# A weight-row sum for attention's values moved into the down stage of the layer before

## The chip, the cores and the metric

The kernel runs on one core of a Trainium2 chip. The metric is the device time of one execution in microseconds (us). Engines are PE (TensorE, matmuls), DVE (VectorE), ACT (ScalarE), POOL (GpSimd) and SP (SyncE, which only issues DMAs here). POOL issues DMAs as well, among them all that add to their destination (`accum_op`).

## The reference

Two layers on `x` (512 rows, width 1024): layer 0 mixes by causal pooling, layer 1 by differential attention with 8 heads, and each is followed by a SwiGLU feed-forward network (FFN) of width 2816.

```
x <- LayerNorm(ALPHA * x + mixer(x));  x <- LayerNorm(ALPHA * x + ffn(x))
attention: q, k, v = split(x @ w_qkv)
  p_c = softmax(q_c k_c^T / 8 + bias[head], causal), c = 0, 1
  o = (p_0 - lam * p_1) @ v;  o <- o * rsqrt(mean(o^2) + eps) * subln_g * (1 - lambda_init);  o @ w_o
ffn: (silu(x @ w_gate) * (x @ w_up)) @ w_down
```

All is float32. The kernel splits each float32 operand into a high and a low part and makes three matmuls for one product.

## The kernel before, in words

The order of all work is written by hand: each engine runs its instructions in program order, and waits stand where a tile isn't ready. [...]

**Weights.** All weights lie in `wall`, in rows of 128 x 1024. `fetch` (L107) loads a row into a `raw` tile on SP's queue (5 buffers). `ready(n)` (L126) splits the next rows up to number n into a pair h, l (6 buffers): ACT casts the high part, DVE subtracts for the low part. For the rows in `by_dma` (most of q's and k's) ACT writes the high part and minus the raw row, and POOL adds the row by an accumulating DMA (L135). Each split also fetches the row five further on.

**Layer 0's FFN.** Its down stage (loop over `DOWN`, L924) is a product by seven part products P1, Q5, P6, Q3, P7, P2, Q4, of six items each. An item needs a weight tile (`fetch_item`, SP, tiles d and r) and a left operand (`left`, L743); those of Q3 and P7 come by POOL's DMAs from `ssum` (L753). `prepare(j + 5, j + 4)` runs five and four items ahead of PE. Between Q4's items stand the norm (`spread_of`, L194, whose power runs on POOL, L199) and the turn of x.

**Attention, values.** The values are also a product by seven part products. Four need sums of weight rows. `tall` is the sum of quarters 0, 1 and 2: SP loads quarter 0 (L1004), POOL adds quarter 1 (L1006) and 2 (L1008); `short`, in `vals`, is the sum of quarters 1 and 2 (L1005, L1007). These five are issued when attention begins. Later POOL adds quarter 3 to `tall` (L1282). On PE the order is P1 (`va`), P2 (`vb`), q and k of head 0, then P6 with `vt` = split `tall`, P7 with `vs` = split `short`, Q4 with `vu` = split `tall` after the last addition. `load_gb(1)` reuses `tall`'s buffer, and SP's fetches stand behind it. `load_bias(0)` (L1103) is issued after Q4's copies, just before the loop over heads.

**Heads.** For each h the loop does `combine(h-1, 3)`, then `root(h-2)` (two matmuls `ss`, ACT's Ln and Exp), `affine` of layer 0's norm (h = 1 to 4), `scaled(h-2)` (DVE multiplies into `rso`, then a split into `heads`), the query product q and its split, the transposes of head h-1, k and its split, `mix(h-1)` (`o`, its square `sq` on ACT, whose split's low part runs on POOL), and four `score_block`s of head h, each with two bias operations on DVE (L1140) and two exponentials on ACT (L1145), with `combine(h, 0..2)` between. Head 1 has Q5 and Q3 of the values besides. `scalars` (h = 0) makes `nlam` from an exponential on ACT. After the loop `gather` multiplies by `w_o`, with `root`, transposes and `mix` of the last heads between.

Of the kernel before, what the change touches and what calls it, by code (L numbers as in the profile page):

```python
# [12 lines left out]
F32 = mybir.dt.float32  # L13
# [3 lines left out]
ALU = mybir.AluOpType  # L17

P = 128
S = 512  # L20
D = 1024
# [33 lines left out]
def trunk(ctx, tc, x, wall, pscale, lam_p, subln, table, lng, lnb, band, first, onehot, out):  # L55
    nc = tc.nc

    keep = ctx.enter_context(tc.tile_pool(name="keep", bufs=1))
# [202 lines left out]
        turned(n, s)  # L261

    flip, flipped = transposed, turned

    lines = dram.tile([HEADS, LINE], F32, name="lines")

# [223 lines left out]
    def ffn(layer, late):  # L490
# [5 lines left out]
        with tc.tile_pool(name=f"ffn{layer}", bufs=1) as fp:  # L496
# [426 lines left out]
            done = store if final else None  # L923
            for p in DOWN:  # L924
                j0 = DOWN.index(p) * len(PAIRS)
                if p in ("P1", "Q5", "P2"):
                    banks[p] = [bank(f"{p}_{layer}_{s}") for s in range(2)]
                accs = banks[{"P1": "P1", "Q5": "Q5", "Q3": "Q5", "P2": "P2"}.get(p, "P1")]
                together = len(PAIRS) - (tail if p == "Q4" else 0)
                for i in range(together):  # L930
                    j = j0 + i
                    prepare(j + 5, j + 4)
                    if p == "Q4":
                        if i == together - 1:
                            prepare(len(items), len(items))
                            ready(c1 + FB + 2)
                        for s in range(2):
                            if i == s:
                                spread_of(n, s)
                            if i == s + 1:  # L940
                                norm(n, s)
                    multiply(j, accs, range(2))
                for s in range(2):
                    if p == "P1":
                        add_to(s, 0, accs[s], ALPHA)
                    elif p == "Q5":
                        add_to(2 + s, 1, accs[s], ALPHA)
                    elif p == "P6":
                        add_to(s, 1, accs[s], ALPHA, op=ALU.subtract)
                    elif p == "Q3":  # L950
                        add_to(s, 1, accs[s])
                        stat(n, s, 1)
                    elif p == "P7":
                        add_to(2 + s, 1, accs[s], op=ALU.subtract)
                        stat(n, 2 + s, 1)
                    elif p == "P2":
                        add_to(s, 0, accs[s])
                        stat(n, s, 0)
                    elif p == "Q4":
                        if s == 0 and not final:  # L960
                            turn(n, 0)
                        for i in range(len(PAIRS) - tail, len(PAIRS)):
                            if final and s == 0:
                                prepare(j0 + i + 5, j0 + i + 5)
                                if i == 1:
                                    spread_of(n, 0)
                                    spread_of(n, 1)
                                if i == 2:
                                    norm(n, 0, done)
                            multiply(j0 + i, accs, (s,))  # L970
                        add_to(2 + s, 0, accs[s], ALPHA)
                        stat(n, 2 + s, 0)
                        spread_of(n, 2 + s)
                        if final and s == 0:
                            norm(n, 1, done)
                        norm(n, 2 + s, done)
                        if not final:
                            if s == 0:
                                turn(n, 1)
                            ready(c1 + FB + 3 + s)  # L980
# [3 lines left out]
    def attention():  # L984
        n = 2
        with tc.tile_pool(name="attn", bufs=1) as ap:
# [8 lines left out]
            nc.gpsimd.memset(ones.bitcast(F32), 1.0)  # L995
            nlam = ap.tile([P, 1], F32, name="nlam")
            vals = ap.tile([P, SB, D], F32, name="vals")
            tall = keep.tile([P, 2, D], F32, tag="gb", name="tall")
            short = vals[:, 2:]

            def two_rows(c):
                return wall[vrow[c] : vrow[c] + 2].rearrange("r p t -> p r t")

            nc.sync.dma_start(out=tall, in_=two_rows(0))  # L1004
            nc.sync.dma_start(out=short, in_=two_rows(1))  # L1005
            nc.gpsimd.dma_start(out=tall, in_=two_rows(1), accum_op=ALU.add)  # L1006
            nc.gpsimd.dma_start(out=short, in_=two_rows(2), accum_op=ALU.add)  # L1007
            nc.gpsimd.dma_start(out=tall, in_=two_rows(2), accum_op=ALU.add)  # L1008

            def quarter_tile(tag, name):  # L1010
                if tag[0] == "p":
# [93 lines left out]
            def load_bias(h):  # L1105
                t = ap.tile([P, S], F32, tag="bias", name=f"bias{h}", bufs=2)
                row = lines[h : h + 1, :]
                nc.sync.dma_start(
                    out=t,
                    in_=bass.AP(  # L1110
                        tensor=row.tensor,
                        offset=row.offset + 1,
                        ap=[[1, P], [1, S]],
                    ),
                )
                biases[h] = t
# [81 lines left out]
            def root(h):  # L1198
                acc, sh, sl = outs[h]
                ss = bank(f"ss{h}")  # L1200
                nc.tensor.matmul(ss, ones, sh, start=True, stop=False)
                nc.tensor.matmul(ss, ones, sl, start=False, stop=True)
                rs = ap.tile([P, S], F32, tag="rso", name=f"rso{h}")
                nc.scalar.activation(rs, ss, AF.Ln, bias=eps_t, scale=1.0 / (2 * HD))
                nc.scalar.activation(rs, rs, AF.Exp, scale=-0.5)
                outs[h] = (acc, rs)

            def scaled(h):
                acc, rs = outs[h]
                nc.vector.scalar_tensor_tensor(rs, acc, gcol, rs, op0=ALU.mult, op1=ALU.mult)  # L1210
                oh, ol = (slots[h if h < 6 else 16 + h][:, i, :] for i in range(2))
                split(oh, ol, rs)
                outs[h] = (oh, ol)
# [34 lines left out]
            def pair_of(name, raw):  # L1248
                h, l = weight_pair(name)
                split(h, l, raw)  # L1250
                return h, l

            flip(1, 2)
            va = [bank(f"va{s}") for s in range(2)]
            w = take(2)
# [54 lines left out]
            for t in (ah, al):  # L1310
                nc.gpsimd.memset(t[:, :P].bitcast(F32), 0.0)

            load_bias(0)
            for h in range(HEADS):
                if h > 0:
                    combine(h - 1, 3)
                if h == 1:
                    vc = [bank(f"vc{s}") for s in range(2)]
                    w = take(2)
                    for r in range(2):  # L1320
                        values("Q5", r, vc, w[r])
                    ready(where[0] + 4)
                    for s in range(2):
                        combined(part(1, 1, s), vc[s], part(1, 1, s), ALU.subtract)
                if h > 0:
                    split_values(h - 1)
                if h > 1:
                    root(h - 2)
                if h == 0:
                    scalars()  # L1330
                if 0 < h <= SB:
                    affine(n - 1, h - 1)
                if h == SB + 1:
                    load_gb(n)
                if h > 1:
                    scaled(h - 2)
                if h + 1 < HEADS:
                    load_bias(h + 1)
                if h > 0:
                    accs = [bank(f"{nm}{h}") for nm in "qk"]  # L1340
                    w = take(2)
                    ready(where[0] + 1)
                    query(accs[0], w[0])
                    split_query(h, "q", accs[0])
                    transposed(h - 1)
                    query(accs[1], w[1])
                    ready(where[0] + 2)
                    split_query(h, "k", accs[1])
                    if h == 1:
                        w = take(2)  # L1350
                        for r in range(2):
                            values("Q3", r, vc, w[r])
                        ready(where[0] + 1)
                        for s in range(2):
                            combined(part(0, 1, s), vc[s], part(0, 1, s), ALU.subtract)
                    ready(where[0] + 3)
                    mix(h - 1)
                start_scores(h)
                score_block(h, 0)
                score_block(h, 1)  # L1360
                if h == HEADS - 1:
                    ready(where[0] + 4)
                combine(h, 0)
                score_block(h, 2)
                combine(h, 1)
                score_block(h, 3)
                combine(h, 2)
# [145 lines left out]
```

## Time and profile before

| | us |
|---|---|
| median of 3 runs | 979.24 |
| lowest and highest | 978.32, 979.27 |
| profiled execution, its own time | 981.04 |
| its span (first to last instruction) | 979.3 |
| PE busy | 935.2 (96%) |
| DVE busy | 786.3 (80%) |
| ACT busy | 515.7 (53%) |
| POOL busy | 127.3 (13%) |

The profile is one execution. A row of the timeline has the start in us from the span's start, the duration, the engine, the line, the operation, and what is written from what is read; in brackets stands the idle time before it and what ended that. A row of the list of waits has the engine and line that waited, what ended the wait, the sum in us, the number of waits and the longest. A row of the stretches has its limits and length, busy time of PE, PE's weight loads, DVE, ACT and POOL with instruction counts, the granted PE clock (1.00 is full), the share of the 16 DMA engines' time in use, and GB/s. A row of DMA issues ends with the size and the time from issue to landing; a queue's row has packets, MB, and the share of the DMA engines' time. Layer 0's down stage lies at 266 to 373 us, the values at 374 to 470, the heads up to about 584.

### The profile page before, as it was taken

How to read it: one execution, taken by the hardware profiler on the slowest of the kernel's cores; microseconds unless marked ns; L12 is line 12 of the kernel's file. 1: busy time of each engine (PE TensorE's matmuls, PEld its weight loads, DVE VectorE, ACT ScalarE, POOL GpSimd, SP SyncE). 2: the span in 40 equal slices, each digit the busy share in tenths (PEclk: the TensorE clock that was granted, in tenths of full speed). 3: DMA queues.
4: the chain of work that ended last, by engine and by line, in shares of the span. 5: the costliest groups of instructions: out<-in, count | busy, mean ns of one | idle time of the engine just before them, and what ended most of it. 6: DMA issues, size and time to landing. Idle time of an engine off the chain costs nothing.

```text
span 979.3 us, 14929 instructions
## 1 busy us (share of the span) xinstructions
PE 935.2 (96%) x5712; PEld 831.6 (85%) x5712; DVE 786.3 (80%) x1157; ACT 515.7 (53%) x820; POOL 127.3 (13%) x153
## 2 busy tenths in 40 slices
PE   9999999999999999378999999999999999999996
PEld 8898899999988888257777788898889999988885
DVE  8869889999887788336678677869969999988778
ACT  6752445545554558254777775473244555554451
POOL 4121111110002002000121110021211110001201
PEclk9999999999999999698999999999999999999999
DMA  8487998876768857763566532288878885877952
GB/s 242 142 265 227 298 294 251 291 239 218 245 215 307 326 188 217 147 184 109 142 142 158 133 105 65 87 256 259 283 211 268 271 246 191 280 246 264 369 179 87
DMA packets 86182, 211.63 MB, mean 216 GB/s; under 512 B 15156, under 2 KB 26676, under 8 KB 86110
## 3 DMA queue, kind: packets, MB, share of 16 engines
q1 hardware_dynamic: 43420, 117.16, 35.7%
q0 software_dynamic: 18912, 58.73, 24.1%
q10 hardware_dynamic: 23778, 34.78, 9.8%
q8 instruction: 45, 0.74, 0.3%
q14 instruction: 27, 0.22, 0.1%
HBM read 173.93 MB, written 36.72 MB: 215 GB/s over the span
## 4 chain that ended last, share of the span: by engine, by line
PE 40%; DVE 8%; issue 4%; ACT 4%; DMA 2%; POOL 0%; DVEq 0%; SPq 0%; ACTq 0%; POOLq 0%
PE A L847 8%; PE P L914 6%; PE C L847 4%; PE Q L914 3%; PE B L847 2%; PE g L149 2%; PE u L151 2%; PE u L149 2%; PE g L151 2%; PE g L150 2%; PE u L150 1%; PE va L1067 1%; DVE p L1140 1%; DVE p L1159 1%; DVE p L1155 1%
## 5 line engine op out<-in xcount | busy, mean ns | idle before, releaser
L593 DVE TENSOR_TENSOR raw<-raw,raw 128x1024 f32<-128x1024 f32 x56 | 68.3, 1219 | 0.5
L123 ACT CAST xs<-hid 128x512 fp32r<-128x512 f32 (+1 forms) x60 | 34.7, 582 | 24.4 <-DVE hid L761 24.4
L1145 ACT ACTIVATE p<-p,mn 128x128 f32<-128x128 f32 (+3 forms) x64 | 35.3, 553 | 22.5 <-DVE mn L1140 22.5
L124 DVE TENSOR_TENSOR xs<-hid,xs 128x512 fp32r<-128x512 f32 (+1 forms) x60 | 38.4, 642 | 7.8 <-ACT xs L123 7.8
L249 ACT ACTIVATE y<-pt,bT,gT 128x128 f32<-128x128 f32 x80 | 30.1, 456 | 19.4 <-PE pt L235 19.4
L1140 DVE CUSTOM_DVE_ANT_0 p<-s,bias 128x128 f32<-128x128 f32 (+3 forms) x64 | 28.1, 486 | 13.8 <-DMA bias<-lines 8.7
L692 POOL DMA_DIRECT2D b<-in_wall x20 | 14.0, 706 | 172.1 <-DVE g_58l L599 65.3
L753 POOL DMA_DIRECT2D xs<-ssum x24 | 17.5, 727 | 141.8 <-PE Q L914 67.9
L199 POOL TENSOR_TENSOR rs<-rs,mhalf 128x1 f32<-128x1 f32 x16 | 12.6, 786 | 169.5 <-DVE rs L198 130.0
L625 DVE TENSOR_TENSOR hid<-sg,u 128x512 f32<-128x512 f32 x16 | 11.0, 686 | 27.3 <-PE u L151 16.5
L692 POOL DMA_DIRECT2D hid<-in_wall x24 | 18.8, 825 | 88.6 <-DMA tsum<-hid 42.3
L729 ACT CAST v<-u 128x512 fp32r<-128x512 f32 x22 | 13.6, 620 | 27.4 <-DVE u L727 27.4
L124 DVE TENSOR_TENSOR xt<-y,xt 128x512 fp32r<-128x512 f32 x20 | 13.6, 690 | 13.5 <-ACT xt L123 13.5
L190 DVE BATCH_NORM_STATS2 st<-res 128x6 f32<-128x512 f32 x32 | 22.2, 695 | 1.1
L873 ACT ACTIVATE sg<-sg 128x512 f32<-128x512 f32 x14 | 8.9, 633 | 25.7 <-DVE sg L866 25.7
L641 ACT CAST xs<-hid 128x1024 fp32r<-128x1024 f32 x8 | 8.4, 1051 | 24.7 <-DVE hid L658 11.6
L693 POOL DMA_DIRECT2D hid<-in_wall x12 | 14.8, 1234 | 47.9 <-DMA hid<-in_wall 43.7
L1067 PE MATMUL va<-vt0h,heads 128*128 128x512 f32 x8 | 4.6, 645 | 15.1 <-DVE vals L1246 15.1
L1159 DVE SCALAR_TENSOR_TENSOR p<-p,sm,p 128x128 f32<-128x128 f32 (+3 forms) x32 | 17.6, 551 | 1.1
L862 DVE TENSOR_TENSOR hid<-C,hid 128x512 f32<-128x512 f32 x14 | 9.7, 691 | 10.7 <-PE C L847 9.1
L858 ACT COPY hid<-C 128x512 f32<-128x512 f32 x14 | 8.2, 588 | 18.5 <-PE C L847 18.5
L693 POOL DMA_DIRECT2D b<-in_wall x10 | 12.3, 1233 | 37.6 <-DMA b<-in_wall 37.6
(1189 smaller groups left out, 3691.1 us busy)
## 6 DMA issues: line engine op xcount, KB each, us to landing
raw<-in_wall SPq DMA_DIRECT2D x122, 512.0 KB, 5.0
r<-tsum SPq DMA_DIRECT2D x40, 512.0 KB, 4.3
hid<-in_wall POOLq DMA_DIRECT2D x36, 512.0 KB, 7.2
b<-in_wall POOLq DMA_DIRECT2D x30, 512.0 KB, 5.8
r<-in_wall SPq DMA_DIRECT2D x30, 512.0 KB, 4.6
tsum<-hid ACTq DMA_DIRECT2D x24, 512.0 KB, 5.6
ssum<-v ACTq DMA_DIRECT2D x22, 512.0 KB, 3.9
tsum<-b ACTq DMA_DIRECT2D x20, 512.0 KB, 4.9
```

Of the source, the lines that this page charges most:

```text
L123: nc.scalar.copy(dst_h, src)
L124: (low or nc.vector).tensor_tensor(dst_l, src, dst_h.bitcast(F32), op=ALU.subtract)
L149: nc.tensor.matmul(acc, ah, bh, start=start, stop=False)
L150: nc.tensor.matmul(acc, ah, bl, start=False, stop=False)
L151: nc.tensor.matmul(acc, al, bh, start=False, stop=stop)
L249: nc.scalar.activation(y[:, k, :], pt[:, k * P : (k + 1) * P], AF.Identity, bias=bT[:, n, kk : kk + 1], scale=gT[:, n, kk : kk + 1],)
L593: tt(t, raws[pair[0]], raws[pair[1]], op=ALU.add)
L692: nc.gpsimd.dma_start(out=t[:, j], in_=src[:, j])
L847: nc.tensor.matmul(o, w[:, c], x[:, kk, :], start=p in ("P1", "Q5", "P2") and f + kk + e == 0, stop=p in ("Q4", "Q3", "P2") and (f, kk, e) ...
L914: nc.tensor.matmul(accs[s], x[:, k, r], y[:, c], start=first and k == 0 and e == 0, stop=last and k == m - 1 and e == 2, skip_group_check= ...
L1140: nc.vector.tensor_tensor_reduce(out=p, in0=accs[c][:, :w], in1=biases[h][:, w - 1 :: -1] if w < S else biases[h][:, ::-1], op0=ALU.add, o ...
L1145: nc.scalar.activation(p, p, AF.Exp, bias=mn[:, q, c : c + 1], scale=-1.0, accum_out=sm[:, q, c : c + 1],)
```

## The change

The load of `tall` and its two additions move from the start of attention into layer 0's down stage: `tall_step` loads quarter 0 ahead of Q3's items, adds quarter 1 ahead of P2's and quarter 2 ahead of Q4's. `short` is made as before. `load_bias(0)` is issued when attention begins, ahead of the turn of the third row block. In the head loop `root(h-2)` moves from ahead of q to behind the transposes, `scaled(h-2)` from ahead of q to behind k's split, and the `ready` calls are set so that, from head 1 on, one row is split ahead of q's split and one ahead of k's, none ahead of `mix`; in the last head two rows instead of one are left for the call between the score blocks.

```diff
+    def two_rows(c):
+        return wall[vrow[c] : vrow[c] + 2].rearrange("r p t -> p r t")
+    talls = []
+    def tall_step(p):
+        if p == "Q3":
+            talls.append(keep.tile([P, 2, D], F32, tag="gb", name="tall"))
+            nc.sync.dma_start(out=talls[0], in_=two_rows(0))
+        elif p in ("P2", "Q4"):
+            nc.gpsimd.dma_start(
+                out=talls[0], in_=two_rows(1 if p == "P2" else 2), accum_op=ALU.add
+            )
...
             for p in DOWN:
                 j0 = DOWN.index(p) * len(PAIRS)
+                if not final:
+                    tall_step(p)
...
-            tall = keep.tile([P, 2, D], F32, tag="gb", name="tall")
+            tall = talls[0]
             short = vals[:, 2:]
-            nc.sync.dma_start(out=tall, in_=two_rows(0))
             nc.sync.dma_start(out=short, in_=two_rows(1))
-            nc.gpsimd.dma_start(out=tall, in_=two_rows(1), accum_op=ALU.add)
             nc.gpsimd.dma_start(out=short, in_=two_rows(2), accum_op=ALU.add)
-            nc.gpsimd.dma_start(out=tall, in_=two_rows(2), accum_op=ALU.add)
...
+            load_bias(0)
             flip(1, 2)
...
-            load_bias(0)
             for h in range(HEADS):
...
-                if h > 1:
-                    root(h - 2)
...
-                if h > 1:
-                    scaled(h - 2)
...
-                    ready(where[0] + 1)
+                    ready(where[0] + (3 if h == 1 else 1))
                     query(accs[0], w[0])
                     split_query(h, "q", accs[0])
                     transposed(h - 1)
+                    if h > 1:
+                        root(h - 2)
                     query(accs[1], w[1])
-                    ready(where[0] + 2)
+                    ready(where[0] + (4 if h == 1 else 2))
                     split_query(h, "k", accs[1])
+                    if h > 1:
+                        scaled(h - 2)
                     if h == 1:
                         w = take(2)
                         for r in range(2):
                             values("Q3", r, vc, w[r])
-                        ready(where[0] + 1)
                         for s in range(2):
                             combined(part(0, 1, s), vc[s], part(0, 1, s), ALU.subtract)
-                    ready(where[0] + 3)
                     mix(h - 1)
```

More of the change, by code (lines that the diff above doesn't have):

```diff
@@ L997, in attention @@
             vals = ap.tile([P, SB, D], F32, name="vals")
-            tall = keep.tile([P, 2, D], F32, tag="gb", name="tall")
+            tall = talls[0]
             short = vals[:, 2:]
-            def two_rows(c):
-                return wall[vrow[c] : vrow[c] + 2].rearrange("r p t -> p r t")
-            nc.sync.dma_start(out=tall, in_=two_rows(0))
             nc.sync.dma_start(out=short, in_=two_rows(1))
-            nc.gpsimd.dma_start(out=tall, in_=two_rows(1), accum_op=ALU.add)
             nc.gpsimd.dma_start(out=short, in_=two_rows(2), accum_op=ALU.add)
-            nc.gpsimd.dma_start(out=tall, in_=two_rows(2), accum_op=ALU.add)
             def quarter_tile(tag, name):
```

## The prediction

> **What bounds the kernel now.** I read the page's slices first, then the list of waits, then the timeline between 372 and 625 us.
>
> ```profile
> span 979.3 us, 14929 instructions
> ...
> PE   9999999999999999378999999999999999999996
> ```
>
> PE is full everywhere but in slices 17 to 19 (24.5 us each), 392 to 465 us, where attention makes the values. A change pays there first; elsewhere it has to shorten PE's own work. The waits of that stretch:
>
> ```profile
> ACT vt0h L123 <- DMA tall<-in_wall: 15.2, 1, 15.2
> ...
> PE q L151 <- DMA w80l<-in_wall: 1.2, 1, 1.2
> ```
>
> ACT's cast of `tall` waits 15.2 us for a transfer. The tile view of `tall` shows why:
>
> ```profile
> L1004 SPq DMA_DIRECT2D tall<-in_wall x1: 378/378/378, 377.6 to 377.6; - x1
> L1006 POOL DMA_DIRECT2D tall<-in_wall x1: 1210/1210/1210, 385.0 to 385.0; - x1
> L1008 POOL DMA_DIRECT2D tall<-in_wall x1: 1179/1179/1179, 398.6 to 398.6; - x1
> ...
> L1282 POOL DMA_DIRECT2D tall<-in_wall x1: 1188/1188/1188, 411.6 to 411.6; - x1
> ...
> DMA to landing us min/median/max: 6.9/8.8/13.0
> ```
>
> A load, an accumulation and a second accumulation follow each other, each after the landing of the last: issues at 377.6, 385.0 and 398.6. PE over both gaps (timeline), and the stretch after the first with its clock:
>
> ```profile
> 396.60 0.39 PE L151 MATMUL k<-xt,w73l 128*128 128x512 f32 x1
> ...
> 412.09 0.77 PE L1067 MATMUL va<-vt0h,heads 128*128 128x512 f32 x1 [15.11 <-DVE vals L1246]
> ...
> 420.48 0.39 PE L1067 MATMUL va<-vs0h,heads 128*128 128x512 f32 x1
> ...
> 425.92 0.39 PE L1067 MATMUL va<-vu0h,xt 128*128 128x512 f32 x1
> ...
> 444.25 0.80 PE L1067 MATMUL vc<-w74h,heads 128*128 128x512 f32 x1 [9.82 <-DVE mn L1140]
> ...
> 452.00 0.39 PE L149 MATMUL q<-xt,w76h 128*128 128x512 f32 x1
> ...
> 410.00:415.00 5.00, 2.91 (x7) 2.36 (x8) 5.00 (x7) 2.76 (x4) 1.19 (x1) 0.50 0.29 38
> ```
>
> The four rows from 412.09 to 444.25 start P6, P7, Q4 and Q5, products of 24 equal matmuls. P7 takes 425.92 - 420.48 = 5.44 us. P6 takes 8.39 and Q5 452.00 - 444.25 = 7.75: both follow a gap, of 15.1 and 9.8 us by the brackets, and the granted clock after the first is 0.50. The DVE releasers only end the chains: the first runs from `tall` over cast and subtraction, the second from the bias, as (2) shows.
>
> **The change part by part.** (1) *`tall` early.* The wait goes, if the sum is there by 396.8, where k ends. ACT could cast `vt` right behind its copies:
>
> ```profile
> 391.68 1.06 ACT L1278 COPY vals<-vb 128x512 f32<-128x512 f32 x2
> ```
>
> From 392.7 two casts and two subtractions of 1.04 to 1.23 us (an estimate from their rows' lengths elsewhere in this stage) end near 396, so P6 starts at once: **+15.1 us**, and P6 then runs at P7's pace: 8.39 - 5.44 = **+2.95**.
>
> [...]
>
> What is late next is `short` for P7 and the third quarter (`vu`) for Q4.
>
> ```profile
> 389.89 1.20 POOL L1007 DMA_DIRECT2D vals<-in_wall  x1 [3.67 <-DMA vals<-in_wall]
> ...
> vals<-in_wall POOLq DMA_DIRECT2D x1, 1024.0 KB, 13.1
> ```
>
> Before, `short`'s load queued behind `tall`'s megabyte on SP; its accumulation began at 389.89 and landed near 403. With `tall` gone the load takes `tall`'s place at 377.6, lands 6.9 later, near 384.5, and its accumulation ends between 393 and 398. P7 is due 5.44 after P6, near 402.3, so 4 us are over. `vu`'s accumulation, issued after the last `vt` subtraction at 396.2, lands with the median's 8.8 near 405, and ACT, with two copies and two casts behind P6, is free for it near 405: I charge **-0.3** (bounds 0 and -4.5, the second worked out in rival 1).
>
> (2) *Bias 0 first.* Its load leaves SP's queue behind two `gb` and four `raw` loads and goes out near 378.
>
> ```profile
> 434.96 0.21 DVE L1029 TENSOR_SCALAR nlam<-le 128x1 f32<-128x1 f32 x1 [4.45 <-ACT le L1028]
> ...
> 443.89 0.29 DVE L1140 CUSTOM_DVE_ANT_0 p<-s,bias 128x128 f32<-128x128 f32 x1 [8.65 <-DMA bias<-lines]
> ```
>
> DVE could start head 0 once `nlam` and one small operation are through, so the 8.65 idle us go, not PE's whole 9.8: PE still waits for `nlam`'s chain on ACT, some 1.2 us. **+8.65**, and Q5 at full clock: 7.75 - 5.44 = **+2.3**. The 256 KB go ahead of two `raw` loads that nobody waits for then.
>
> (3) *The transfers in the down stage.* SP loads `tall` after its loads up to the second item of P7, near 312 (its buffer was `b`'s, whose sums SP has read back by then, so the d-tile loads behind it don't wait); POOL issues the first accumulation behind the last `left`, the second when the first has landed. Nothing on PE is queued behind them, but they share the DMA engines.
>
> ```profile
> 310.23 9.09 SPq L530 DMA_DIRECT2D r<-tsum  x6
> ...
> 320.00:325.00 5.00, 5.00 (x23) 4.14 (x23) 2.45 (x2) 1.86 (x2) 1.28 (x2) 1.00 1.03 404
> ...
> 321.88 0.72 POOL L753 DMA_DIRECT2D xs<-ssum  x1 [1.32 <-PE Q L914]
> ...
> q0 software_dynamic: 272, 1.05, 44.7%
> ...
> 329.05 1.21 DVE L124 TENSOR_TENSOR d_28l<-r,d_28h 128x1024 fp32r<-128x1024 f32 x1
> ...
> L914 PE MATMUL P<-d_28h,xs x16: 389/389/389, 337.1 to 939.2; 128*128 128x512 f32 x16
> ```
>
> The first row holds P7's six loads, `tall` goes between the second and the third. The engines are full at 320 (share 1.03, 404 GB/s), so 1.05 MB plain costs 2.6 us of them. The queue's row is the lone accumulation between 411 and 424: 44.7% of 13 us, 5.8 us for 1.05 MB. In all 2.6 + 2 x 5.8 = 14.2 us of engine time are added. The cover: item 28 is split by 330.26 and needed at 337.1, 6.8 us of slack. `tall`'s load uses 2.6 of it, and the accumulations start only when the last lefts are through, near 329, when the stage asks less of the queues. I take **0** (bounds 0 and -10, rival 2).
>
> (4) *Heads.* `ready` now makes the weights of the next q at the start of a head, so w80 is there in head 2: +1.2; the two matmuls of `root` stay (0.46, below) behind the transposes: **+0.75**. For the later heads (timeline; the two rows of L1170 are from the chain of waits):
>
> ```profile
> 490.78 0.62 ACT L1194 ACTIVATE sq<-o 128x512 f32<-128x512 f32 x1
> ...
> 529.18 0.63 ACT L1194 ACTIVATE sq<-o 128x512 f32<-128x512 f32 x1
> ...
> 582.25 0.60 ACT L1194 ACTIVATE sq<-o 128x512 f32<-128x512 f32 x1 [0.44 <-PE o L151]
> ...
> 556.19 0.98 PE at L1170 x7
> ...
> 573.75 0.99 PE at L1170 x7
> ...
> 580.89 0.69 DVE L124 TENSOR_TENSOR heads<-k,heads 128x512 fp32r<-128x512 f32 x1 [1.29 <-ACT heads L123]
> ...
> 574.22 0.74 DVE L1210 SCALAR_TENSOR_TENSOR rso<-o,gcol,rso 128x512 f32<-128x512 f32 x1
> ...
> 588.46 0.39 PE L1201 MATMUL ss<-sqh,ones 128*128 128x512 f32 x1
> ...
> 588.92 0.40 PE L149 MATMUL wo<-w95h,heads 128*128 128x512 f32 x1
> ```
>
> From square to square, heads 3 and 4 take (529.18 - 490.78) / 2 = 19.2 us, heads 5 to 7 17.7. The long ones have `affine` on DVE ahead of `scaled`, q's and the transposes' splits, and ACT behind them; that goes, as `scaled` no longer holds q's split. The short ones are ruled by a ring: the last `combine` lets the transposes of 573.75 through, then k, mix, square, exponentials, `combine`: 573.75 - 556.19 = 17.56. The change puts two things on that ring. `root`'s matmuls stand between transposes and k: 588.92 - 588.46 = 0.46. And `scaled`'s multiply and cast stand between k's split and the square: by the rows of head 7 DVE ends k's low part near 581.5, multiplies 0.65 to 0.74, ACT casts 0.6, so the square starts near 582.8, not 582.25: 0.55. The ring becomes 18.57. Heads 3 and 4 gain 2 x 0.63, heads 5 to 7 lose 3 x 0.88: **-1.4** (bounds: +3.7 if neither is on the ring, -6.4 if both cost double). The fetches and accumulations that `ready` issues move with it on SP and POOL, ahead of nothing that is due:
>
> ```profile
> w82l<-in_wall POOLq DMA_DIRECT2D x1, 512.0 KB, 10.6
> ```
>
> From the end of ACT's part, 0.8 us after the transposes are let through, to the next q's first low weight lie k, mix, scores and root, about 11 us; the longest such flight is 10.6, so the cover is thin, and each us beyond costs one in five heads. What gets shorter, the wait of `root` for POOL's square split, was on PE ahead of q; PE now waits as long at the transposes.
>
> (5) *Tail.* `ready` is one row later in head 7: w94 is cast where w95 was, w95 behind it.
>
> ```profile
> 585.72 0.39 PE L149 MATMUL wo<-w94h,heads 128*128 128x512 f32 x1
> ...
> 586.24 1.22 DVE L124 TENSOR_TENSOR w95l<-raw,w95h 128x1024 fp32r<-128x1024 f32 x1 [2.06 <-ACT w95h L123]
> ```
>
> w94's low part is then ready at 587.46 by the square's clock, and PE wants it 0.23 after 585.72, some 0.55 earlier now: a stall of 2.05 less those 0.55, **-1.5** (bounds 0 and -2.5).
>
> **Sum**: 15.1 + 2.95 + 8.65 + 2.3 - 0.3 + 0 + 0.75 - 1.4 - 1.5 = 26.55. The profiled execution took 981.04 us, its span 979.3 and 1.74 around it; it would take 954.5. It stands 1.8 above the median of the three runs, 979.24, which becomes **952.7**.
>
> **The rivals.** 1. *`short` takes `tall`'s place* (the wait moves, so the change does less than it says). If `short` still lands at 403, as with 13.1 us behind other traffic, ACT casts it to 405, P7 waits 2.9 us, and `vu`, behind it in POOL's queue, reaches Q4 at 412.3 instead of 407.8: 4.5 lost, **957.2**. For it: accumulations took up to 13.0. Against: its load loses a megabyte ahead of it.
>
> 2. *The down stage starves.* If SP's loads yield for the whole 14.2 us of (3), less 6.8 of slack, PE stalls 7.4 us and loses another 2.3 to 2.95 at half clock: **962.7**. For it: share 1.03 when `tall` starts. Against: two thirds of the added work comes after the lefts. [...]
>
> 3. *Neither addition is on the ring*: five heads at 17.56, 5 x 1.01 better, **947.7**.
>
> 4. *Slower: POOL's queue blocks the norm.*
>
> ```profile
> 360.47 0.95 POOL L199 TENSOR_TENSOR rs<-rs,mhalf 128x1 f32<-128x1 f32 x1 [37.87 <-DVE rs L198]
> ```
>
> The norm's power of layer 0 stands on POOL behind the second accumulation, which waits for the first's landing. If that comes after 359.2, the norm, the turn and P1 slip one for one; it eats the whole gain from 386 on, 63 us after an issue near 322.7; at 390 it gives **983.5**. For it: the order of the queue. Against: the longest flight is 13.1, so 37 us are over.
>
> **How the numbers follow.** Forecast 59%, rivals 12%, 11%, 10% and 8%. Its own range, with the small bounds of (1), (4) and (5), is 950 to 957. The range reaches to rival 3, takes in rival 1 and the nearer half of rival 2: 947 to 961. About 0.2% can be told from no change here; all but rival 4 are faster by more: 0.92 faster, 0.01 within, 0.07 slower.
>
> **What would show it.** Right: no wait of ACT on `tall` above 1 us, P6, P7 and Q4 back to back at 5.44 each, DVE's first bias operation right after `nlam`, Q5 at 5.44, squares 18.6 us apart in all heads from 3 on, a PE wait near 2 us for w94l. Wrong: PE waits on d-tiles between 312 and 372, ACT's wait for `vals` (rival 1), squares 17.6 apart (rival 3), a late POOL power (rival 4).

## The result and the profile after

| | before | forecast | after |
|---|---|---|---|
| median, us | 979.25 | 952.7 (947 to 961) | 955.52 |
| profiled execution, its own time, us | 981.04 | 954.5 | 955.08 |
| its span, us | 979.3 | 952.75 | 953.3 |

The ratio of the times is 0.9763, 95% interval 0.9737 to 0.9789: faster, inside the range. The two spans differ by 26.0 us, where the sum said 26.55. The page of the changed kernel, its slices (line numbers from 264 on have moved by 5 to 16; `tall`'s load, L1004, is now L273, its additions, L1006 and L1008, are L275):

```profile
span 953.3 us, 14919 instructions
...
PE   9999999999999999999999999999999999999996
...
PEclk9999999999999999999999999999999999999999
```

The three slices of 3, 7 and 8 tenths are gone. Tile view of `tall`, after:

```profile
L275 POOL DMA_DIRECT2D tall<-in_wall x2: 1208/1218/1227, 324.5 to 337.7; - x2
L273 SPq DMA_DIRECT2D tall<-in_wall x1: 384/384/384, 312.7 to 312.7; - x1
L123 ACT CAST vt0h<-tall x1: 1058/1058/1058, 393.8 to 393.8; 128x1024 fp32r<-128x1024 f32 x1
```

Load at 312.7, additions at 324.5 and 337.7, cast at 393.8 with nothing to wait for. PE's timeline after, the first matmuls of P6, P7, Q4, Q5 and of head 1's q:

```profile
397.96 0.47 PE L1076 MATMUL va<-vt0h,heads 128*128 128x512 f32 x1
403.52 0.39 PE L1076 MATMUL va<-vs0h,heads 128*128 128x512 f32 x1
408.96 0.39 PE L1076 MATMUL va<-vu0h,xt 128*128 128x512 f32 x1
418.53 0.50 PE L1076 MATMUL vc<-w74h,heads 128*128 128x512 f32 x1 [1.06 <-DVE mn L1149]
424.14 0.39 PE L149 MATMUL q<-xt,w76h 128*128 128x512 f32 x1
```

P6 has no idle time ahead of it; P6, P7 and Q5 take 5.56, 5.44 and 5.61 us; 1.06 us of wait are left ahead of Q5, on `nlam`'s chain. And the heads and the tail after: three of ACT's last four squares, then PE's last wait at the transposes and the two at the tail's weights:

```profile
517.81 0.59 ACT L1203 ACTIVATE sq<-o 128x512 f32<-128x512 f32 x1
...
554.85 0.59 ACT L1203 ACTIVATE sq<-o 128x512 f32<-128x512 f32 x1
577.44 0.60 ACT L1203 ACTIVATE sq<-o 128x512 f32<-128x512 f32 x1 [3.76 <-PE o L151]
```

```profile
545.38 0.98 PE L1179 MATMUL at<-ident,p 128*128 128x128 f32 x7 [0.94 <-DVE p L1168]
...
558.85 0.50 PE L149 MATMUL wo<-w94h,heads 128*128 128x512 f32 x1 [0.37 <-ACT w94h L123]
...
560.11 0.50 PE L150 MATMUL wo<-w94l,heads 128*128 128x512 f32 x1 [0.76 <-DVE w94l L124]
```

Squares are 18.52 us apart (two periods from 517.81 to 554.85; forecast 18.57), the last stretch, with w94 late, takes 22.59 (21.35 before). What the sum has against it, term by term, from the starts in the two traces:

| term | forecast | measured |
|---|---|---|
| wait ahead of P6 | +15.1 | +15.26 |
| P6 at full clock | +2.95 | +2.83 |
| `vu` for Q4 | -0.3 | 0 |
| wait ahead of Q5 | +8.65 | +8.75 |
| Q5 at full clock | +2.3 | +2.14 |
| down stage | 0 | -0.43 |
| head 2 | +0.75 | +0.68 |
| heads 3 and 4 | +1.26 | +1.35 |
| heads 5 to 7 | -2.64 | -2.47 |
| tail | -1.5 | -1.24 |
| elsewhere: FFN ahead of the down stage, rest after the tail | 0 | -0.70, -0.20 |
| sum | 26.55 | 25.97 |

The 0.70 lies ahead of every instruction that the change moves. It is the profiled run of before that was quick there: the down stage begins 0.27 to 1.2 us later in the trace of every other run told here.

### The profile page after: what moved, and what is told of

It reads as the page before. It is cut to its first block, busy times and chain, and to the rows that moved or that the text cites. A ratio compares the mean times of both kernels' runs of the same rounds, so it can differ in the third digit from the quotient of the medians.

```text
span 953.3 us, 14919 instructions
## 1 busy us (share of the span) xinstructions
PE 931.9 (98%) x5712; PEld 829.2 (87%) x5712; DVE 785.1 (82%) x1157; ACT 515.4 (54%) x820; POOL 127.3 (13%) x153
## 4 chain that ended last, share of the span: by engine, by line
PE 78%; DVE 12%; ACT 4%; DMA 4%; issue 2%; POOL 0%; DVEq 0%; ACTq 0%; POOLq 0%
PE A L861 17%; PE P L928 9%; PE C L861 8%; PE B L861 4%; PE Q L928 3%; PE g L151 3%; PE u L150 3%; PE u L149 3%; PE u L151 3%; PE g L150 3%; PE g L149 3%; PE va L1076 2%; DMA r<-in_wall 2%; PE k L151 2%; PE k L150 2%
## 5 line engine op out<-in xcount | busy, mean ns | idle before, releaser
L706 POOL DMA_DIRECT2D b<-in_wall x20 | 14.0, 705 | 171.0 <-DVE g_58l L613 66.0
L124 DVE TENSOR_TENSOR heads<-k,heads 128x512 fp32r<-128x512 f32 x7 | 4.8, 692 | 20.4 <-ACT heads L123 20.4
L1144 PE MATMUL s<-heads 64*128 64x256 f32 (+2 forms) x168 | 18.4, 337 | 0.3
L1168 DVE SCALAR_TENSOR_TENSOR p<-p,sm,p 128x128 f32<-128x128 f32 (+3 forms) x32 | 17.7, 552 | 1.1
```

What stands on the lines that cost most here:

```text
L124: (low or nc.vector).tensor_tensor(dst_l, src, dst_h.bitcast(F32), op=ALU.subtract)
L706: nc.gpsimd.dma_start(out=t[:, j], in_=src[:, j])
```

## Experiments

All were timed in five rounds (the five accumulations in three) beside the kernel before on the same chip, whose medians there were 980.04 to 980.31.

| kernel | median, us | ratio, 95% interval |
|---|---|---|
| `tall` alone | 965.48 | 0.9852 (0.9835 to 0.9868) |
| bias 0 alone | 971.16 | 0.9907 (0.9890 to 0.9923) |
| both, heads as before | 953.88 | 0.9736 (0.9722 to 0.9751) |
| changed kernel again | 956.37 | 0.9758 (0.9744 to 0.9771) |
| split order of heads | 952.03 | 0.9715 (0.9700 to 0.9731) |
| `root` back | 953.00 | 0.9728 (0.9715 to 0.9741) |
| `affine` apart | 948.15 | 0.9678 (0.9665 to 0.9691) |
| `affine` whole | 957.17 | 0.9770 (0.9746 to 0.9795) |
| five accumulations | 968.18 | 0.9885 (0.9868 to 0.9902) |
| load later | 954.58 | 0.9743 (0.9729 to 0.9756) |
| `nlam` early | 954.70 | 0.9742 (0.9729 to 0.9755) |
| three edits together | 946.33 | 0.9658 (0.9645 to 0.9671) |

### One part alone: `tall`, bias 0, both without the heads

The kernel before with `tall_step` and `tall = talls[0]` alone:

> The kernel before with the row sum of three quarters made in layer 0's down stage, and nothing else of the change. My theory: the terms add up, so this gives the wait before P6 (15.3 us between the two traces), P6's half clock (2.8) and takes 0.4 for a stall at d-item 30: 979.25 - 17.7 = 961.5 us, Q5 still waits 9.8 us for the bias. Rival (the bias comes late by SP's queue at a time of its own and takes the place of the wait for tall): Q5's gap grows from 9.8 towards 27 us and the time stays above 972.

The kernel before with the bias alone:

```diff
+            load_bias(0)
             flip(1, 2)
...
-            load_bias(0)
             for h in range(HEADS):
```

> The kernel before with bias 0 loaded first in the attention's queue, and nothing else of the change. My theory: Q5's wait falls from 9.8 to 1.06 us and Q5 runs at full clock (2.14): 979.25 - 10.9 = 968.35 us. Rival (Q5 is slow for another reason than the gap, since the gap of 15 us before P6 stays): only the wait goes, 970.5. Rival (the accumulations of tall and short hold DVE's inputs back anyway): above 975.

Both parts, the loop over heads as before:

> The changed kernel with the heads as before: tall early and bias 0 first, but root and scaled ahead of q and ready in its old places. My theory, by the squares of the two traces: the seven heads take 110.68 instead of 111.13 us and the tail 21.35 instead of 22.59, so 955.5 - 1.7 = 953.8 us; the third part of the change costs time as a whole. Rival (the new order was needed once bias and tall are early): equal or slower, 955.5 to 958.

PE's timeline of `tall` alone, Q5's first matmul and q's:

```profile
428.58 0.80 PE L1076 MATMUL vc<-w74h,heads 128*128 128x512 f32 x1 [9.88 <-DVE mn L1149]
...
436.89 0.39 PE L149 MATMUL q<-xt,w76h 128*128 128x512 f32 x1
```

The bias comes as late after Q4 as before (9.88 against 9.82): its load, which SP issues at 431.06 in the kernel before, behind four `raw` loads, hangs on the casts that free the `raw` buffers and moves with them, so the wait for it doesn't take `tall`'s place. The time is 4 us above the 961.5 expected; 0.8 of that is the group, in which the kernel before took 980.04. In the trace the first square is at 456.47, so 15.1 us earlier than before, and the 2.6 that are missing there of 17.7 are these: the FFN ahead began the down stage 1.20 later, PE lost 1.18 at item 30 (0.43 in the changed kernel, which the 17.7 allow for), Q5 took 8.31 instead of 7.75. PE's timeline of bias 0 alone:

```profile
413.71 0.76 PE L1067 MATMUL va<-vt0h,heads 128*128 128x512 f32 x1 [16.17 <-DVE vals L1246]
...
436.90 0.50 PE L1067 MATMUL vc<-w74h,heads 128*128 128x512 f32 x1 [1.07 <-DVE mn L1140]
...
442.51 0.39 PE L149 MATMUL q<-xt,w76h 128*128 128x512 f32 x1
```

Q5's wait falls to 1.07 and Q5 to 5.61 us, as expected; the wait for `tall` is 16.17 instead of 15.11. With `tall` still on the path there, this us and 0.57 in the FFN ahead take most of the difference between the 10.9 expected and the 9.5 us by which the first square comes earlier. Both together, 953.88, beat the changed kernel by 1.6 to 2.5 us by the medians (the intervals just overlap); in the trace heads and tail are 0.55 and 1.27 shorter than after. So two parts bring the whole gain, and the third costs about what the sum said, 2.15 (1.8 in the two traces).

### The ring of the heads

Old order in heads 5 to 7, and w94 in time:

```diff
+                if h > 4:
+                    root(h - 2)
...
+                if h > 4:
+                    scaled(h - 2)
...
-                    if h > 1:
+                    if 1 < h < 5:
                         root(h - 2)
...
-                    if h > 1:
+                    if 1 < h < 5:
                         scaled(h - 2)
...
+                    if h == HEADS - 1:
+                        ready(where[0] + 3)
                     mix(h - 1)
```

> The changed kernel with its own order of root and scaled in heads 2 to 4 and the old one (both ahead of q) in heads 5 to 7, and in head 7 one more weight made ready before the mix. My theory (root and scaled stand on the ring): heads 5 to 7 go from 18.5 to 17.5 to 18.0 us from square to square, -2.5 in all, and w94 is there in time, -1.24: 955.5 - 3.7 = 951.8 us. Rival (the ring is 18.5 because of something else, such as ready's early transfers): the squares stay 18.5 apart and only the tail gains, 954.3.

`root` ahead of q again in all heads, `scaled` left behind k's split:

> The changed kernel with root back ahead of q in every head, scaled left behind k's split. My theory (the prediction's sum: root's two matmuls add 0.46 to the ring, scaled's multiply and cast 0.55): squares 18.53 - 0.46 = 18.07 us apart, six heads, 955.5 - 2.8 = 952.7 us. Rival 1 (root alone makes the ring long, because k and the mix stand behind it): 17.6 apart, 950. Rival 2 (scaled alone makes it long, root's matmuls only fill a wait): 18.5 apart, 955.5.

Three of ACT's squares of the split order, the first two three periods apart and the last behind the tail's weights, and two of `root` back:

```profile
501.58 0.59 ACT L1203 ACTIVATE sq<-o 128x512 f32<-128x512 f32 x1
...
554.16 0.60 ACT L1203 ACTIVATE sq<-o 128x512 f32<-128x512 f32 x1 [0.45 <-PE o L151]
575.53 0.60 ACT L1203 ACTIVATE sq<-o 128x512 f32<-128x512 f32 x1 [3.67 <-PE o L151]
```

```profile
498.49 0.59 ACT L1203 ACTIVATE sq<-o 128x512 f32<-128x512 f32 x1
516.56 0.59 ACT L1203 ACTIVATE sq<-o 128x512 f32<-128x512 f32 x1
```

17.52 apart in the old order, 18.07 with `scaled` alone behind k's split, 18.52 with both: each addition is on the ring, with 0.55 and 0.45 us where the prediction put 0.55 and 0.46. The tail of the split order is 21.37 again, so the 1.24 us were the late w94.

Why were heads 2 to 4 long before? `affine` was taken apart (left out here: its new argument, the old places of `root` and `scaled`, and the `ready` ahead of the last `mix`, which is as in the split order):

```diff
+                if h > 1:
+                    root(h - 2)
...
-                if 0 < h <= SB:
-                    affine(n - 1, h - 1)
...
+                if h > 1:
+                    scaled(h - 2)
+                if 0 < h <= SB:
+                    affine(n - 1, h - 1, (0,))
...
                     transposed(h - 1)
...
+                    if h <= SB:
+                        affine(n - 1, h - 1, (1,))
```

> The changed kernel with root and scaled ahead of q in all heads as before, ready as in the change (in head 7 one weight more ahead of the mix), and affine's two operations of 1.22 us taken apart on VectorE: the multiply behind scaled, the addition behind the transposes' splits, where VectorE waited 1.7 and 1.4 us for ScalarE. My theory (the old order was slow in heads 2 to 4 only because 2.45 us of affine stood ahead of scaled and of q's split): squares 17.5 apart in all heads, 3.0 less than with the split order, 952.0 - 3.0 = 949.0 us. Rival (the slow heads of before come from a weight cast ahead of the square, or from affine at any place on VectorE): 18.5 to 19.2 apart in heads 2 to 4, 952 to 954.

and put back whole, ahead of `scaled`:

> The kernel with root and scaled ahead of q and affine taken apart (948.15 us, squares 17.5 apart), with affine whole again at its old place, ahead of scaled. It tells apart what made heads 2 to 4 of the kernel before 19.2 us long. Theory 1 (affine's 2.45 us on VectorE hold scaled, its cast and with them q's and the transposes' splits): squares of heads 2 to 4 from 18.5 to 19.2 apart, 948.15 + 3 to 5 = 951 to 953 us. Theory 2 (the third weight of a head, which ready cast ahead of the square, made them long; it isn't cast there here): squares 17.5 apart, 948 us.

Two of ACT's squares with `affine` apart, two periods (heads 3 and 4) between them, and ACT in head 4 with `affine` whole:

```profile
462.98 0.60 ACT L1202 ACTIVATE sq<-o 128x512 f32<-128x512 f32 x1 [0.59 <-PE o L151]
...
498.08 0.60 ACT L1202 ACTIVATE sq<-o 128x512 f32<-128x512 f32 x1 [0.62 <-PE o L151]
```

```profile
483.32 0.63 ACT L1203 ACTIVATE sq<-o 128x512 f32<-128x512 f32 x1
...
496.57 0.62 ACT L123 CAST heads<-rso 128x512 fp32r<-128x512 f32 x1 [3.67 <-DVE rso L1219]
497.10 1.05 ACT L133 CAST w86h<-raw 128x1024 fp32r<-128x1024 f32 x1
498.05 1.05 ACT L134 ACTIVATE w86l<-raw 128x1024 fp32r<-128x1024 f32 x1
499.01 0.57 ACT L118 ACTIVATE heads<-q 128x512 fp32r<-128x512 f32 x1
...
503.06 0.63 ACT L1203 ACTIVATE sq<-o 128x512 f32<-128x512 f32 x1
```

Apart: 17.5 in every head, 948.15 us. Whole: 19.19, 19.72 and 19.74 in heads 2 to 4 and 20.14 in head 5, 957.17, so 9 us for the place of two operations of 1.22. ACT waits 3.67 us for `scaled`, which stands behind `affine` on DVE; only then come the weight's two casts and q's. Theory 1 holds in kind and was too small in size (3 to 5 expected): it left out the two casts behind the late one, 2.1 us, and what they delay: head 5 has no `affine`, but PE waits 2.12 there, at 509.31, for w86's low part. Theory 2 isn't needed: no third weight is cast ahead of the square here, and the heads are long all the same.

### The down stage

Five accumulations, to put a price on rival 4 (the kernel then computes another sum and serves for its time alone):

```diff
-            nc.gpsimd.dma_start(
-                out=talls[0], in_=two_rows(1 if p == "P2" else 2), accum_op=ALU.add
-            )
+            for _ in range(1 if p == "P2" else 4):
+                nc.gpsimd.dma_start(
+                    out=talls[0], in_=two_rows(1 if p == "P2" else 2), accum_op=ALU.add
+                )
```

> The changed kernel with five accumulations onto tall in the down stage instead of two (the third row three times more, so the sum is another one). It measures rival 4 of the prediction: the norm's power stands on POOL behind the last accumulation. My theory: they start at 324.5, 337.7, 350, 362 and 374, POOL cannot reach the power of 363 before 375, the norm slips 12 us and with it the turn: about 967 us. Rival (a DMA that waits holds only its queue, not POOL): 956 to 958, the power at 363 as in the changed kernel. If the three more also starve d-tiles, PE waits there between 350 and 362 as well.

POOL's timeline of that kernel, then DVE's rows that make the power's input and read its result:

```profile
371.31 1.19 POOL L276 DMA_DIRECT2D tall<-in_wall  x1 [9.26 <-DMA tall<-in_wall]
372.06 1.04 POOL L199 TENSOR_TENSOR rs<-rs,mhalf 128x1 f32<-128x1 f32 x1
```

```profile
367.20 0.15 DVE L198 TENSOR_SCALAR rs<-mv 128x1 f32<-128x1 f32 x1
...
373.14 0.81 DVE L208 TENSOR_SCALAR res<-res,mv,rs 128x1024 f32<-128x1024 f32 x1 [4.57 <-POOL rs L199]
```

The power, at 363.02 in the changed kernel, comes at 372.06, right behind the last accumulation, and the time is 968.18. Its input was ready at 367.35, so POOL held it for 4.7 us: the accumulation ahead of it waited 9.26 us for a landing, and nothing behind it on POOL ran. Rival 4's mechanism is real. The other half of the 9.0 us, 4.4, is not POOL's: the input itself is that much later than in the changed kernel, mostly because ACT waits 4.11 us for item 39's weight tile. With two accumulations POOL had 25 us to spare.

`tall`'s load six items later:

```diff
-        if p == "Q3":
+        if p == "P7":
```

> The changed kernel with tall's first load six items later in SP's queue (with P7 instead of Q3), so near 329 instead of 312.7; the accumulations then start near 341 and 353. My theory (d-item 30 stalls PE by 0.4 to 1.2 us because load and first accumulation share the DMA engines with the loads of items 26 to 30, in the stretch where the share is full already): the stall goes and nothing is late, since the sum lands near 366 and is cast at 394: 955.5 - 0.9 = 954.6 us. Rival (the stall moves to items 32 to 36): 955.5 or more. Rival (POOL's power waits for the second accumulation): 957 and more.

First the kernel before: ACT's cast of item 26 and the low part of item 30's left operand on DVE.

```profile
321.55 1.05 ACT L123 CAST d_26h<-r 128x1024 fp32r<-128x1024 f32 x1 [1.58 <-DMA r<-tsum]
...
334.03 0.68 DVE L124 TENSOR_TENSOR xs<-hid,xs 128x512 fp32r<-128x512 f32 x1
```

Then the changed kernel: ACT's casts of items 26 and 28, two stretches, the second one's DMA queues (q0 is POOL's), and DVE and PE at item 30.

```profile
326.65 1.05 ACT L123 CAST d_26h<-r 128x1024 fp32r<-128x1024 f32 x1 [6.50 <-DMA r<-tsum]
...
332.84 1.05 ACT L123 CAST d_28h<-r 128x1024 fp32r<-128x1024 f32 x1 [2.44 <-DMA r<-tsum]
```

```profile
320.00:325.00 5.00, 5.00 (x24) 4.14 (x23) 1.23 (x1) 0.14 (x1) 1.95 (x3) 1.00 1.03 407
...
330.00:335.00 5.00, 5.00 (x23) 4.14 (x23) 4.50 (x6) 1.45 (x2) 0.00 (x0) 1.00 1.06 254
...
q0 software_dynamic: 193, 0.79, 78.5%
q1 hardware_dynamic: 199, 0.49, 27.9%
```

```profile
341.85 0.68 DVE L124 TENSOR_TENSOR xs<-hid,xs 128x512 fp32r<-128x512 f32 x1
...
342.06 0.39 PE L928 MATMUL P<-d_30l,xs 128*128 128x512 f32 x1
342.58 0.73 PE L928 MATMUL P<-d_30h,xs 128*128 128x512 f32 x2
```

The stage itself begins 0.70 us later in this trace, which the next numbers leave out. Item 26's cast comes 4.4 us later than before, and the first addition, issued at 324.49, had then been out for 2 us only: most of this is the load. Item 28's cast is 5.3 us later, the end of its split (335.42 instead of 330.26) 4.5, so 2.3 of its 6.8 us of slack are left. What comes too late is item 30's left operand: its low part stands behind item 31's weight on ACT and DVE, whose load is late too. It ends 7.1 us later, at 342.53 instead of 334.71, where it had 6.9 to spare, and PE loses 0.43 us. The nine other traces with this place of the load lose 0.55 to 1.55 there; the one with `affine` apart, 1.0 there, loses 1.5 more at the norm, where PE waits 1.36 us for DVE. With the load later, POOL's timeline:

```profile
347.03 1.21 POOL L275 DMA_DIRECT2D tall<-in_wall  x1 [10.78 <-DMA tall<-in_wall]
360.74 0.95 POOL L199 TENSOR_TENSOR rs<-rs,mhalf 128x1 f32<-128x1 f32 x1 [12.50 <-DVE rs L198]
```

Both additions run 9 to 11 us later (335.02 and 347.03), the power isn't held, and PE loses nothing at any item of the stage. The median is 954.58, where 954.6 was expected; against the changed kernel's two medians that is 0.9 and 1.8 less, with overlapping intervals, so the stall's end is shown by the trace, its worth in the median is not.

### What is left, and the three together

The changed kernel was timed again beside the last two:

> The changed kernel unchanged, timed beside the other two of this group on one chip. Theory: 955.5 us, the ratio to before within its first interval of 0.9737 to 0.9789.

`nlam`'s chain earlier:

```diff
             split_query(0, "k", accs[1])
+            scalars()
...
-                if h == 0:
-                    scalars()
```

> The changed kernel with the chain of nlam (two small reductions, the table load of 1.28 us, an exponential) behind the split of k of head 0, where ScalarE waits 2.9 us for P6, instead of behind Q4's copies. My theory: DVE's first bias operation no longer waits for nlam, PE's wait of 1.06 us at Q5 goes, and with it Q5's slow clock, which cost 1.6 us in about half of the traces: 955.5 - 1.06 - 0.8 = 953.6 us, Q5 always at 5.4 to 5.6. Rival (the wait moves to the exponentials or to Q5's weights w74): 955 to 955.5. Rival (the table load delays P6's copies and so Q4's weights): slower than 955.5.

PE's timeline of it, Q5's first matmul and q's first two rows with a wait or without:

```profile
417.69 0.50 PE L1076 MATMUL vc<-w74h,heads 128*128 128x512 f32 x1
...
423.28 0.39 PE L149 MATMUL q<-xt,w76h 128*128 128x512 f32 x1
...
424.68 0.50 PE L151 MATMUL q<-xt,w76l 128*128 128x512 f32 x1 [0.79 <-DMA w76l<-in_wall]
```

The wait ahead of Q5 is gone, Q5 takes 5.59, and 0.79 of it comes back at once: q of head 1 is there earlier, its first low weight (a POOL accumulation) is not. 954.70 beside 956.37, 1.7 us, with intervals that overlap.

`affine` apart, load later and `nlam` early in one kernel:

> The changed kernel with three edits together: root and scaled ahead of q with affine taken apart (948.15 alone), tall's first load six items later (0.9 better alone), nlam's chain early (theory 1.9). My theory: they touch different stretches and add up, 948.15 - 0.9 - 1.9 = 945.4 us. Rival (gains of one stage are given back in the next): 947 to 948.

946.33, 0.9 above the sum, of which 0.74 are the same wait for w76's low part. It beats the kernel before by 3.4% and the changed one (0.9758, interval from 0.9744) by 1.0%.

## Why the prediction was right, point by point

1. **`tall` early: right.** The wait for `tall` went whole (+15.26), P6, P7 and Q4 stand back to back, `short` was 0.69 us late for ACT, which cost PE nothing. Rival 1 did not occur: nothing took the wait's place, in the changed kernel or with `tall` alone.
2. **Bias 0: right.** DVE's first bias operation is at 418.19, right behind `nlam` at 418.00; PE's 1.06 us that stay were forecast as 1.2. The clock term, 2.14 in this trace, was partly luck: five of ten traces with this wait lose 1.6 us of it, see the last section.
3. **The down stage: the step that failed.** "I take 0" rested on `tall`'s load using 2.6 us of item 28's slack and on the accumulations coming near 329, "when the stage asks less of the queues". With the load ahead of it, item 26 was 4.4 us late, the first addition came at 324.5 (rival 4 itself had 322.7), and the engines stayed full to 350 (shares 1.02 to 1.06, where before had 0.93, 0.66 and 0.34 from 330 to 345). Nor was item 28 the place that gives way first: it kept 2.3 us, and item 30's left operand ran out. The stall of rival 2 was there, and 0.43 to 1.55 us was its price (2.5 in all in the one trace where the norm was hit too), not 10. Why the load cost 4.4 and not 2.6 is open.
4. **Heads: right, and for the reason given.** The period, both additions to the ring and the cause of the long heads were each tried alone. Rival 3 is refuted: at 17.5 the squares stand only when neither is on the ring, which needs the old order and `affine` out of the way. `ready`'s thin cover for the next q held. One detail was off: PE's waits at the transposes are 5.8 us in six heads, not as long as those of `root` before, which were 3.8.
5. **Tail: right.** PE's stall was 0.37 + 0.76 at w94, and it goes when w94 is split a call earlier.
6. **Rival 4: not here, but real**, as the five accumulations show. Its room was overstated: from 322.7 to 359.2 are 37 us, but the flight of 13.1 belongs in them, which leaves 23; measured, the second addition went out 25 us ahead of the power.
7. **From the profile to the median: the larger part of the miss.** The spans differ by 26.0, the medians by 23.7 and, in the second timing, 23.8. The forecast took 1.8 off because the profiled run of before stood that far above its median; the changed kernel's stands 0.4 below its own. One reason that the runs show: the changed kernel lost Q5's clock in one of its two traces and not in the other, 1.6 us, and the profiled run of the result is the one that kept it, while both traces with the gap of 9.8 us lose it. The rest of the step is open.

The two clock terms were read from rows of before, as 2.95 and 2.3; measured, they are 2.83 and 2.14. The kernel before shows where they come from; here are the two stretches at half clock around P6's and Q5's start:

```profile
401.12:418.19 17.07, 6.10 (x14) 4.79 (x15) 8.16 (x9) 4.85 (x6) 1.19 (x1) 0.50 0.60 112
...
438.67:448.91 10.24, 4.66 (x11) 3.70 (x12) 4.83 (x21) 3.36 (x13) 0.00 (x0) 0.50 0.62 184
```

The full clock came back 6.10 and 4.66 us after PE's first matmul (PE's busy time in these rows), each about twice its term.

## What to carry to other kernels

Sum a change by the gap it closes, the clock that comes back behind it (2.83 and 2.14 us here) and the wait that is next in line, and try each term alone: here two of three parts brought it all, and the third cost 2 us. An operation moved behind a split or a transpose is only free if it isn't on the ring that sets the period; the starts of one instruction from head to head show that at once. Slack read at one tile is not the slack of the stage: here item 28's weight kept 2.3 of its 6.8 us, and a left operand two items on, split behind a later weight, ran out.

## What the runs showed of the hardware

**A wait of 1.06 or 1.07 us cost the clock in five traces and not in five others.** With bias 0 early and `nlam` late, ten traces have the same wait ahead of Q5, 1.06 or 1.07 us. In five Q5 then takes 5.57 to 5.61 us, in the other five 7.17 to 7.21: 1.6 us more. The same four us of the changed kernel and of both parts with the heads as before, with the granted clock as third number from the right:

```profile
419.00:423.00 4.00, 4.00 (x19) 3.25 (x18) 3.81 (x17) 2.68 (x11) 0.00 (x0) 1.00 1.06 275
```

```profile
419.00:423.00 4.00, 4.00 (x11) 3.17 (x12) 3.81 (x17) 3.02 (x12) 0.00 (x0) 0.57 1.06 274
```

The 33 waits of 0.94 to 1.02 us at the heads' transposes, in six traces, never did that: behind each of the six in the changed kernel the granted clock is 1.00 over the next four us. So it isn't the length of the wait alone, which is the same in all ten traces. What decides was not shown, as no run moved the wait on purpose.

**An accumulation held the DMA engines longer for its bytes than the plain loads beside it.** Between 330 and 335 us in the changed kernel, POOL's queue, by then almost only the first addition, moved 0.79 MB in 78.5% of the engines' time, the plain loads 0.49 MB in 27.9%: 201 GB/s of full engines against 351. The stretch as a whole moved 254 GB/s at a share of 1.06, where the one at 320 moved 407 at 1.03.
